# Block copies of turned squares on ScalarE instead of GpSimd, in a two-layer decoder trunk

## The chip, the cores and the metric

The kernel runs on one core of one Trainium2 chip. The metric is the device time of one execution in microseconds; the time before is the median of three runs, 2173.76 us (2171.62 to 2175.25).

## The reference

A decoder trunk of two layers on 256 tokens of width 2048, in fp32. Each layer is a token mixer and a gated feed-forward block with a short convolution:

```
h = h + gla_mixer(h, ...)                    # layer 0: gated linear attention, 4 heads
h = h + conv_ffn(h, ...)
k_blk, v_blk, k_mean = shared_kv(h, ...)     # layer 1: attention with 16 heads, causal, one block of 256
h = h + moba_mixer(h, ...)
h = h + conv_ffn(h, ...)

def conv_ffn(x, norm_w, w_up, conv_w, conv_b, w_down):
    h = rms_norm(x, norm_w) @ w_up           # (256, 2048) @ (2048, 11264)
    hp = pad(h, 2 rows in front)
    acc = conv_b
    for j in range(3): acc = acc + conv_w[j] * hp[:, j:j + S]
    a, u = split(acc, 2, axis=-1)
    return (silu(a) * u) @ w_down            # (256, 5632) @ (5632, 2048)
```

The convolution runs over tokens, and the products with the weights run over features.

## The kernel before

**Weights.** Every weight is streamed once from HBM, in chunks of 128 x 2048 fp32 (`wraw`, three buffers, loads on SyncE's queue, line L107). A chunk is two halves of 128 x 1024. For each half ScalarE makes a rounded high part (`whi`, L145), and VectorE subtracts it from the half to make the low part (`wlo`, L147). Both have four buffers. TensorE multiplies with the high part (L382), then with the low part (L385). One half is one step: `step` calls the jobs that are due, `WeightStream.prefetch` issues the parts some two halves ahead, and the products of the half follow.

**Groups.** `gemm_tok` makes a group of 512 output columns for both 128-token tiles, tokens on partitions, in eight steps of 12 matmuls. `ffn` has 22 groups in each layer (`up`); the gate of layer 0 has three such groups (`gate`), and each layer's output projection three (`out`).

**The turn.** What follows needs features on partitions and tokens along the free dimension. So after a group `turn_up` copies its two PSUM tiles to `up` on ScalarE (L761), VectorE transposes each in blocks of 32 x 32 (`uT`, L763), and `square` moves the blocks to their places: 16 copies, each from one 32-partition row of blocks to another, 32 x 256 elements (L395), on GpSimd. In [128, 2, 512] that is one copy for each pair of source quadrant m and target quadrant c. `squares` does the same for `gate` and `out` (L402). With three gate groups, six out groups and 44 up groups there are 53 x 16 = 848 copies.

**After the turn.** Eight and eleven steps later `conv` works on the two halves of the group: on ScalarE a scaled copy (`au`, L776), on VectorE two multiply-adds for each of two rows (L781, L783); one step on `gate` does the Silu on ScalarE (L789), the product on VectorE (L791), a rounded copy on ScalarE (`hid`, L423) and the subtraction on VectorE (L424). For some groups VectorE also makes sums of these (`comb`, L712 to L715), and GpSimd's queue stores them (`aside`, L735).

**Sums made ahead.** The down projection uses sums of weight blocks. `make_ahead` loads a chunk every nine steps (`ahead`, L333, SyncE's queue), VectorE makes four sums in it (L330, L331), and GpSimd's queue stores it (`tsum`, L340).

**What sets the order.** Each engine takes its instructions in order. A scheduler places them by priority from the program's order; `after_high()` and `after_low()` tell it to put an instruction behind the latest high or low part that was issued:

```
    def after_high():
        return tc.issue_after(ws.high.ins)
```

Waits between engines are by semaphores, in the order of each queue.

Of the kernel before, what the change touches and what calls it, by code (L numbers as in the profile page):

```python
# [159 lines left out]
def trunk(ctx: ExitStack, tc: tile.TileContext, xT, cst, msk, w1p, w2a, w_k, w_qa, w_v2, w_v, w_gt, w_g, w_got, w_go,  # L160
          w_up0, w_dn0, w_kk, w_kv, w_mq, w_mot, w_mo, w_up1, w_dn1, rel, onehot, out):
    nc = tc.nc
    V, A, T = nc.vector, nc.scalar, nc.tensor
# [181 lines left out]
    def after_high():  # L345
        return tc.issue_after(ws.high.ins)
# [43 lines left out]
    def square(y, x):  # L390

        for m in range(4):
            xs_ = x[32 * m:32 * m + 32].rearrange("a t (n c b) -> a n t c b", c=4, b=32)
            for c in range(4):
                nc.gpsimd.tensor_copy(y[32 * c:32 * c + 32, :, :, 32 * m:32 * m + 32], xs_[:, :, :, c])  # L395

    def squares(name, xs):

        x, y = slot([128, 2, 512], F32, name + "T"), slot([128, 4, S], F32, name)
        for t in range(2):  # L400
            with after_low():
                V.transpose(x[:, t], xs[t])  # L402
        square(y.rearrange("p n (t s) -> p n t s", t=2), x)
        return y
# [343 lines left out]
    def ffn(layer, nrm, then):  # L748
# [6 lines left out]
        def turn_up(g, ps):  # L755

            x = slot([128, 2, 512], F32, "uT")
            us = [temp("up", (128, 512)) for _ in range(2)]
            for t in range(2):
                with after_high():  # L760
                    A.activation(us[t], ps[:, t, :], AF.Copy, scale=nrm.col[:, t:t + 1])  # L761
                with after_low():
                    V.transpose(x[:, t], us[t])  # L763
            y = slot([128, 2, 2, S], F32, "up")
            square(y.rearrange("p j i (t s) -> p (j i) t s", t=2), x)
            for jj in range(2):
                after(UP_LAG[jj], lambda jj=jj: conv(g, jj, y[:, jj]))
# [505 lines left out]
```

## Time and profile before

| | |
|---|---|
| runs | 2171.62, 2173.76, 2175.25 us; median 2173.76 |
| profiled execution, first to last instruction (span) | 2171.2 us; no other time is given for it |
| TensorE (PE) busy | 2162.0 us, 9936 matmuls |
| VectorE (DVE) busy | 1839.8 us |
| ScalarE (ACT) busy | 1301.2 us |
| GpSimd (POOL) busy | 771.9 us |
| the 704 up copies on POOL (L395) | 521.2 us busy, mean 740 ns, 391 at the least and 1469 at the most |
| granted TensorE clock | 1.000 |

The span is what the timeline and the windows count from; the fastest run is 0.4 us above it. A busy share is a mean over the span: TensorE is near 100% in every slice of the page. A row of a group names line, engine, operation, written and read tiles and shapes, then busy time, mean duration, and the engine's idle time before it with what ended that.

### The profile page before, as it was taken

To read this page: it belongs to the slowest core of one execution; us is meant where nothing else is said; L and a number is where in the kernel's file an instruction comes from. 1 tells how busy PE (TensorE), PEld (TensorE's weight loads), DVE (VectorE), ACT (ScalarE), POOL (GpSimd) and SP (SyncE) were. 2 spreads that over 40 slices of the span, in tenths; PEclk is the share of its full clock that TensorE was granted. 3 is DMA by queue.
4 is the path that set the end of the run, shared out by engine and by line. 5 is a ranking of instruction groups with operands and counts; after the bars stand their busy time and mean duration, and the time that the engine had idled before them with its cause. 6 is when DMAs were issued, how large, how long until landed. Compare 5 with 4: busy or idle time off the path is not lost.

```text
span 2171.2 us, 28783 instructions
## 1 busy us (share of the span) xinstructions
PE 2162.0 (100%) x9936; PEld 1800.0 (83%) x9936; DVE 1839.8 (85%) x2525; ACT 1301.2 (60%) x1840; POOL 771.9 (36%) x1069
## 2 busy tenths in 40 slices
PE   9999999999999999999999999999999999999998
PEld 7888888888888888887888888888888888888887
DVE  6686788799999897978968787588999999979798
ACT  6655545556565655766756666455565656567575
POOL 0000347364656464300001343153555565552000
PEclk9999999999999999999999999999999999999999
DMA  7575577877778785887967788767788878759896
GB/s 287 210 291 210 217 280 284 325 265 283 275 284 309 275 311 192 328 329 260 367 246 291 276 300 292 254 253 286 279 308 284 305 279 296 290 191 352 323 359 248
DMA packets 113525, 612.99 MB, mean 282 GB/s; under 512 B 29361, under 2 KB 29889, under 8 KB 49634
## 3 DMA queue, kind: packets, MB, share of 16 engines
q1 hardware_dynamic: 94610, 523.75, 66.4%
q0 software_dynamic: 18048, 86.60, 10.5%
q8 instruction: 78, 1.28, 0.2%
q10 hardware_dynamic: 720, 0.79, 0.1%
q14 instruction: 69, 0.57, 0.1%
HBM read 535.31 MB, written 75.78 MB: 281 GB/s over the span
## 4 chain that ended last, share of the span: by engine, by line
PE 97%; DMA 1%; DVE 1%; issue 0%; ACT 0%; ACTq 0%; DVEq 0%
PE acc L382 46%; PE acc L385 23%; PE acc L844 13%; PE p L844 5%; PE acc L367 5%; PE acc L369 2%; DMA ahead<-tsum 1%; DMA wraw<-w_dn 1%; PE sT L594 0%; DVE wlo L147 0%; PE tr L1046 0%; PE s L1064 0%; DMA h<-xT 0%; ACT whi L145 0%; PE z L500 0%
## 5 line engine op out<-in xcount | busy, mean ns | idle before, releaser
L147 DVE TENSOR_TENSOR wlo<-wraw,whi 128x1024 fp32r<-128x1024 f32 (+1 forms) x788 | 959.8, 1226 | 251.7 <-ACT whi L145 202.7
L145 ACT CAST whi<-wraw 128x1024 fp32r<-128x1024 f32 (+1 forms) x788 | 795.5, 1016 | 608.7 <-PE acc L382 434.5
L382 PE MATMUL acc<-whi,xw 128*128 128x512 f32 x3520 | 873.0, 390 | 0.6 <-DVE xw L262 0.6
L382 PEld LDWEIGHTS acc<-whi,xw 128*128 128x128 f32 x3520 | 659.3, 188 | 138.0 <-issue 1.3
L395 POOL COPY up<-uT 32x256 f32<-32x256 f32 x704 | 521.2, 740 | 297.2 <-DVE uT L763 234.6
L385 PE MATMUL acc<-wlo,xw 128*128 128x512 f32 x1760 | 472.5, 389 | 0.0
L385 PEld LDWEIGHTS acc<-wlo,xw 128*128 128x128 f32 x1760 | 330.1, 188 | 68.6 <-DVE wlo L147 0.3
L340 POOL DMA_DIRECT2D tsum<-ahead x58 | 31.6, 545 | 453.0 <-DVE ahead L331 433.5
L844 PE MATMUL acc<-whi,hid 128*128 128x512 f32 x588 | 168.1, 390 | 1.7 <-ACT whi L145 1.7
L147 DVE TENSOR_TENSOR wlo<-ahead,whi 128x1024 fp32r<-128x1024 f32 x98 | 120.0, 1231 | 19.1 <-ACT whi L145 10.7
L844 PEld LDWEIGHTS acc<-whi,hid 128*128 128x128 f32 x588 | 109.8, 188 | 25.2 <-ACT whi L145 2.8
L382 PE MATMUL acc<-whi,xkv 128*128 128x512 f32 x512 | 129.9, 391 | 0.0
L145 ACT CAST whi<-ahead 128x1024 fp32r<-128x1024 f32 x98 | 101.5, 1052 | 42.1 <-PE p L844 16.6
L844 PE MATMUL p<-whi,hid 128*128 128x512 f32 x356 | 111.6, 389 | 0.0
L382 PEld LDWEIGHTS acc<-whi,xkv 128*128 128x128 f32 x512 | 95.1, 188 | 18.9
L844 PE MATMUL acc<-whi,comb 128*128 128x512 f32 x348 | 101.3, 390 | 0.5 <-ACT whi L145 0.5
L844 PE MATMUL acc<-wlo,hid 128*128 128x512 f32 x294 | 96.3, 390 | 0.0
L776 ACT ACTIVATE au<-up,cs 128x256 f32<-128x256 f32 x176 | 95.8, 593 | 0.0
L783 DVE SCALAR_TENSOR_TENSOR au<-up,cs,au 128x254 f32<-128x254 f32 x176 | 89.7, 540 | 0.0
L781 DVE SCALAR_TENSOR_TENSOR au<-up,cs,au 128x255 f32<-128x255 f32 x176 | 89.0, 542 | 0.2
L331 DVE TENSOR_TENSOR ahead<-ahead 128x512 f32<-128x512 f32 x116 | 87.0, 750 | 0.3
L330 DVE TENSOR_TENSOR ahead<-ahead 128x512 f32<-128x512 f32 x116 | 86.9, 750 | 0.3
(282 smaller groups left out, 2363.6 us busy)
## 6 DMA issues: line engine op xcount, KB each, us to landing
wraw<-w_up SPq DMA_DIRECT2D x176, 1024.0 KB, 5.5
ahead<-w_dn SPq DMA_DIRECT2D x58, 1024.0 KB, 8.8
tsum<-ahead POOLq DMA_DIRECT2D x58, 1024.0 KB, 8.3
ahead<-tsum SPq DMA_DIRECT2D x49, 1024.0 KB, 6.8
wraw<-w_dn SPq DMA_DIRECT2D x58, 768.0 KB, 6.2
wraw<-w_dn SPq DMA_DIRECT2D x30, 1024.0 KB, 6.3
wraw<-w_mq SPq DMA_DIRECT2D x16, 1024.0 KB, 5.0
wraw<-w_kk SPq DMA_DIRECT2D x16, 1024.0 KB, 5.3
```

Source lines behind the costliest of these rows:

```text
L145: self.high = nc.scalar.copy(hi[:, a:b], src[:, a:b])
L147: self.low = nc.vector.tensor_sub(lo[:, a:b], src[:, a:b], hi[:, a:b].bitcast(F32))
L330: jobs = [lambda: V.tensor_sub(b22, b22, b12), lambda: V.tensor_sub(b12, b12, b11), lambda: V.tensor_add(b11, b22, b11), lambda: V.tensor_ ...
L331: lambda: V.tensor_add(b11, b22, b11), lambda: V.tensor_sub(b21, b21, b11)]
L367: T.matmul(ps[:, b, :], two[i][0][:, c:c + 128], xs(kt), start=kt == 0, stop=False)
L382: T.matmul(ps[:, t, :], xs(kt)[:, x0 + 128 * t:x0 + 128 * t + 128], hi[:, c:c + 512], start=kt == 0 and x0 == 0, stop=False)
L385: T.matmul(ps[:, t, :], xs(kt)[:, 128 * t:128 * t + 128], lo[:, c:c + 512], start=False, stop=kt == KT - 1)
L395: nc.gpsimd.tensor_copy(y[32 * c:32 * c + 32, :, :, 32 * m:32 * m + 32], xs_[:, :, :, c])
L776: A.activation(au[:, i, :], t[:, i, :], AF.Identity, bias=col(cb + n), scale=col(cw + 2 * 2 * FT + n))
L781: V.scalar_tensor_tensor(au[:, i, 1:], t[:, i, :S - 1], col(cw + 2 * FT + n), au[:, i, 1:], op0=OP.mult, op1=OP.add)
L783: V.scalar_tensor_tensor(au[:, i, 2:], t[:, i, :S - 2], col(cw + n), au[:, i, 2:], op0=OP.mult, op1=OP.add)
L844: T.matmul(p[n], x[xi], w[wi][:, 512 * f:512 * f + 512], start=n not in begun, stop=left[n] == 0)
```

## The change

The 16 copies of `square` are issued to ScalarE, each behind the latest high part.

```diff
         for m in range(4):
             xs_ = x[32 * m:32 * m + 32].rearrange("a t (n c b) -> a n t c b", c=4, b=32)
             for c in range(4):
-                nc.gpsimd.tensor_copy(y[32 * c:32 * c + 32, :, :, 32 * m:32 * m + 32], xs_[:, :, :, c])
+                with after_high():
+                    A.copy(y[32 * c:32 * c + 32, :, :, 32 * m:32 * m + 32], xs_[:, :, :, c])
```

Every line behind it has a number one higher in the changed kernel (L395 is L396, L423 is L424, L776 is L777).

ScalarE's queue around the turn of the twentieth up group of layer 0; the `up` rows are the copies out of PSUM, `au` and `hid` belong to earlier groups. Before:

```order
L145 CAST whi<-wraw 128x1024
L761 ACTIVATE up<-acc,col_h 128x512 x2
L789 ACTIVATE au<-au 128x256
L145 CAST whi<-wraw 128x1024
L776 ACTIVATE au<-up,cs 128x256 x2
L423 CAST hid<-au 128x256
L145 CAST whi<-wraw 128x1024
L789 ACTIVATE au<-au 128x256
L145 CAST whi<-wraw 128x1024 x2
```

The same place in the changed kernel:

```order
L145 CAST whi<-wraw 128x1024
L762 ACTIVATE up<-acc,col_h 128x512 x2
L790 ACTIVATE au<-au 128x256
L145 CAST whi<-wraw 128x1024
L777 ACTIVATE au<-up,cs 128x256 x2
L396 COPY up<-uT 32x8x32 x16
L424 CAST hid<-au 128x256
L145 CAST whi<-wraw 128x1024
L790 ACTIVATE au<-au 128x256
L145 CAST whi<-wraw 128x1024 x2
```

The 16 copies stand in one piece between two casts; the `hid` cast and the next high part are behind them.

VectorE's queue at the same turn, from the low part ahead of the transposes. Before:

```order
L147 TENSOR_TENSOR wlo<-wraw,whi 128x1024
L763 STREAM_TRANSPOSE uT<-up 128x512 x2
L791 TENSOR_TENSOR au<-au 128x256
L147 TENSOR_TENSOR wlo<-wraw,whi 128x1024
L781 SCALAR_TENSOR_TENSOR au<-up,cs,au 128x255 x2
L424 TENSOR_TENSOR hid<-au,hid 128x256
L783 SCALAR_TENSOR_TENSOR au<-up,cs,au 128x254
L147 TENSOR_TENSOR wlo<-wraw,whi 128x1024
L783 SCALAR_TENSOR_TENSOR au<-up,cs,au 128x254
L147 TENSOR_TENSOR wlo<-wraw,whi 128x1024
```

The same place in the changed kernel:

```order
L147 TENSOR_TENSOR wlo<-wraw,whi 128x1024
L764 STREAM_TRANSPOSE uT<-up 128x512 x2
L792 TENSOR_TENSOR au<-au 128x256
L147 TENSOR_TENSOR wlo<-wraw,whi 128x1024
L782 SCALAR_TENSOR_TENSOR au<-up,cs,au 128x255 x2
L784 SCALAR_TENSOR_TENSOR au<-up,cs,au 128x254 x2
L425 TENSOR_TENSOR hid<-au,hid 128x256
L147 TENSOR_TENSOR wlo<-wraw,whi 128x1024
L792 TENSOR_TENSOR au<-au 128x256
L147 TENSOR_TENSOR wlo<-wraw,whi 128x1024 x2
L425 TENSOR_TENSOR hid<-au,hid 128x256
L147 TENSOR_TENSOR wlo<-wraw,whi 128x1024 x3
```

The first `hid` subtraction, which needs ScalarE's `hid` cast, has moved behind all four multiply-adds; the second low part after the transposes stands behind it.

## Prediction

> **What bounds the kernel now.** I read the page's busy times and chain first, then PE's list of waits.
>
> ```profile
> PE 2162.0 (100%) x9936; PEld 1800.0 (83%) x9936; DVE 1839.8 (85%) x2525; ACT 1301.2 (60%) x1840; POOL 771.9 (36%) x1069
> PE 97%; DMA 1%; DVE 1%; issue 0%; ACT 0%; ACTq 0%; DVEq 0%
> PE acc L844 <- ACT whi L145: 2.3, 4, 1.5
> PE junk L219 <- POOL idle L216: 1.3, 1, 1.3
> PE acc L385 <- DVE wlo L147: 0.7, 1, 0.7
> PE acc L382 <- DVE xw L262: 0.6, 1, 0.6
> PE acc L382 <- ACT whi L145: 0.3, 1, 0.3
> ```
>
> A row of waits gives us in total, times, and the longest. PE is busy 2162.0 of 2171.2 us and all its waits together are 5.2 us. No edit that leaves the products alone can win more than the 9.2 us in which PE is idle, and most of that is not behind these copies. The question is whether the moved work makes PE wait. 704 of the 848 copies belong to the 44 groups of the two up projections, so I read one group in the timeline, and the window 410 to 870, which holds 21.
>
> ```profile
> 410.00:870.00 460.00, 460.00 (x2031) 381.04 (x2030) 417.90 (x574) 276.03 (x394) 259.37 (x362) 1.00 0.75 275
> 627.01 1.04 ACT L145 CAST whi<-wraw 128x1024 fp32r<-128x1024 f32 x1
> 627.29 1.98 PE L382 MATMUL acc<-whi,xw 128*128 128x512 f32 x8
> 627.54 1.30 DVE L763 STREAM_TRANSPOSE uT<-up 128x512 f32<-128x512 f32 x2
> 628.97 12.73 POOL L395 COPY up<-uT 32x256 f32<-32x256 f32 x16 [7.43 <-DVE uT L763]
> 629.31 1.06 ACT L145 CAST whi<-wraw 128x1024 fp32r<-128x1024 f32 x1 [0.26 <-PE acc L382]
> 629.66 1.41 DVE L147 TENSOR_TENSOR wlo<-wraw,whi 128x1024 fp32r<-128x1024 f32 x1
> 630.01 1.98 PE L382 MATMUL acc<-whi,xw 128*128 128x512 f32 x8
> ```
>
> In the window row the columns after the length are PE, PEld, DVE, ACT, POOL: PE 460.00 of 460, DVE 417.90 (91%), ACT 276.03 (60%), POOL 259.37 (56%). PE's steps start 2.72 us apart (627.29, 630.01), so a group of eight is 21.76 us. The cast at 629.31 starts as PE ends the high products at 629.27: with four buffers it writes the high part for four steps on. ACT is thus as far ahead as the buffers let it, and it can be held for a while before PE notices.
>
> **Part 1: POOL loses the copies.** POOL's 12.73 us of each group go; nothing waits for POOL in PE's list, so this alone is worth nothing to PE. Its stores of `ahead` and `aside`, which stood behind copies, are issued sooner: nothing again, a buffer is free earlier. What it does change is DVE:
>
> ```profile
> L147 DVE TENSOR_TENSOR wlo<-wraw,whi 128x1024 fp32r<-128x1024 f32 x168 | 221.9, 1322 | 41.3 <-ACT whi L145 39.5 <-PE acc L385 1.3
> L330 DVE TENSOR_TENSOR ahead<-ahead 128x512 f32<-128x512 f32 x30 | 24.0, 800 | 0.1
> L331 DVE TENSOR_TENSOR ahead<-ahead 128x512 f32<-128x512 f32 x32 | 25.4, 794 | 0.1
> L714 DVE TENSOR_TENSOR comb<-au 128x128 f32<-128x128 f32 x9 | 4.3, 478 | 0.0
> L781 DVE SCALAR_TENSOR_TENSOR au<-up,cs,au x176: 467/480/648, 427.5 to 1969.9; 128x255 f32<-128x255 f32 x176
> 398.66 2.35 DVE L147 TENSOR_TENSOR wlo<-wraw,whi 128x1024 fp32r<-128x1024 f32 x2
> 601.88 0.68 DVE L330 TENSOR_TENSOR ahead<-ahead 128x512 f32<-128x512 f32 x1
> 607.02 0.38 DVE L791 TENSOR_TENSOR au<-au 128x256 f32<-128x256 f32 x1
> 642.89 0.41 DVE L424 TENSOR_TENSOR hid<-au,hid 128x256 fp32r<-128x256 f32 x1
> ```
>
> Beside a POOL copy a wlo takes 1.41 (629.66), away from one two take 2.35 together, 1.22 and then 1.13; an `ahead` sum takes 0.80 on average and 0.68 alone. So without POOL DVE gets shorter. An L781 takes 0.47 at the least and 0.65 at the most, a multiply (L791) alone 0.38, a hid subtraction 0.41. In a row I take 0.08 off each, as the two wlo show: a wlo 1.14, an `ahead` sum 0.60, an L781 or L783 0.40, the transposes (1.30 the pair) 1.26, a multiply 0.30, a hid subtraction 0.34. One group without `ahead` work is then 8 x 1.14 + 1.26 + 4 x 0.40 + 2 x 0.30 + 2 x 0.34 = 13.3 us; with 62/21 = 2.9 `ahead` sums (1.8) and the sums of `comb` (nine of L714, and of each of its like, in 21 groups: 0.6 on average), 15.7; waits are not in it. That is a relief of 2 to 3 us a group, and it pays for part of what follows.
>
> **Part 2: ACT gets 16 copies in one piece.** The nearest rows for one copy:
>
> ```profile
> L568 ACT COPY kie<-kie 128x256 f32<-128x256 f32 x4 | 1.6, 406 | 4.1 <-DVE kie L567 4.1
> L423 ACT CAST hid<-au 128x256 fp32r<-128x256 f32 x88 | 35.5, 403 | 71.7 <-DVE au L791 71.7
> L776 ACT ACTIVATE au<-up,cs 128x256 f32<-128x256 f32 x176 | 95.8, 593 | 0.0
> 624.88 1.09 ACT L776 ACTIVATE au<-up,cs 128x256 f32<-128x256 f32 x2
> 66.13 0.40 ACT L507 CAST zst<-zaug 17x256 fp32r<-17x256 f32 x1
> 66.55 0.41 ACT L508 CAST zst<-zaug 17x256 fp32r<-17x256 f32 x1
> ```
>
> 256 elements take 0.40, on 128 partitions or 17. Usually the next instruction overlaps by 0.1 (two L776 of 0.593 in 1.09), which would make the block 16 x 0.31 = 5.0 us. But L507 and L508, which wait for nothing between them, start 0.42 apart, more than the 0.40 of the first: L508 writes from partition 32, L507 from 0. Every one of the 16 copies writes at another block of 32 partitions than the one before. I take 16 x 0.43 = 6.9 us. Bounds: 5.0, and 8.0 if pieces of 32 elements cost 0.50. The Trainium skill, "VectorE: DVE Perf Modes", section "Two Vector instructions with no wait between them", says that a VectorE instruction whose output starts in another 32-partition quadrant is held until the earlier ones end; it says so of VectorE only, the L507 and L508 rows say it of ScalarE.
>
> ACT's total is no problem: 276.03/21 = 13.1 us a group, plus 6.9, is 20.0 of 21.76. What counts is what stands behind the block in ACT's queue: the cast that makes the next high part. Count from the end of a group's last step. The last cast ahead of the block is of the fifth part on; it may start when PE has done the next step's high products, at 2.0, takes 0.96, and two L776 take 1.0: the copies start at 4.0. They end at 10.9, the hid cast at 11.2, the next cast at 12.25. PE wants that part, the sixth, after five steps, at 13.6. The margin is 1.35 us, for a group that begins on time, so one block alone does not stop PE. Two loops decide whether groups begin on time.
>
> **Part 3: the loop through DVE.** When the transposes are done, DVE has on average some 3.5 us to do and then waits for the hid cast behind the block. The copies run 6.9, the hid cast 0.3, the next cast 1.05, and then DVE still has seven wlo (8.0), a multiply (0.3), a hid subtraction (0.3), four L781/L783 (1.6) and the transposes (1.3) before the next block may start: 8.25 + 11.5 = 19.8 us with no `ahead` work, 2.0 below 21.76. Four `ahead` sums (2.4) and the `aside` sums (1.3) make 23.5, 1.7 above. The average group is 19.8 + 1.9 = 21.7: the loop is full. What is over in one group is carried to the next; counted through the 44 groups in their order, group by group with these prices, it passes the margin in five groups by 0.01 to 0.7 us, together 1.4, and by 2.4 in the eleventh, where only a multiply and a `comb` sum stand between DVE's transposes and its wait. Together 4 us. Bounds: nothing at 0.31 a copy; at 0.50 every group is about 1.0 over, 44 us.
>
> **Part 4: the loop through the loads.** `wraw` has three buffers of two parts; one comes free when DVE has made its second wlo. The first wlo behind the block is such a one. The last row is for w_up.
>
> ```profile
> wraw<-w_up SPq DMA_DIRECT2D x176, 1024.0 KB, 5.5
> ahead<-w_dn SPq DMA_DIRECT2D x58, 1024.0 KB, 8.8
> SPq L107 <- DVE wlo L147: 1673.7, 386, 8.6
> DMA to landing us min/median/max: 4.7/5.5/11.4
> ```
>
> SP's queue waits for these wlo all the time (1673.7 us in all), so a later wlo is a later load. Loop: copies 6.9, hid cast 0.3, cast 1.05, wlo 1.14, load 5.5, cast 1.05, wlo 1.14, four L781/L783 1.6, wlo 1.14, transposes 1.3: 21.1 us, 0.6 below the group. A load beside an `ahead` load (8.8) makes 24.4, 2.7 over, of which the margin of 1.35 takes half. Of four loads in a group one is in the loop, and an `ahead` load falls in three groups of four: I take one group in five, 44 x 0.2 x 1.35 = 12 us. Bounds: nothing (every such load 4.7 to 5.5), and 44 us (every such load half-way between the two rows, 7.15, so that the loop is 22.75 and each group 1.0 over).
>
> **The nine other blocks** (gate and out) have the same 6.9 us in ACT, beside fewer ACT and DVE instructions; margins of 1.3 us or more by the same count. I cost them at nothing; if PE's steps there show waits, 9 x 1 us at most.
>
> **Sum.** 4 + 12 = 16 us on the profiled execution, whose span of 2171.2 stands beside the fastest of the three runs (2171.62; the median is 2.6 above the span). 2171.6 + 16 = 2188 us. 0.2%, some 4.3 us, is about what a measurement of this kernel tells from no change.
>
> **Rivals.** *Hidden* (no change): the copies overlap by 0.1 as L776 does, or loads land in 5.5. Block 5.0, DVE loop 19.8 on the average group, load loop 19.2; no term left, 2172 to 2178. For it: wherever ACT stays on the same partitions its rows overlap; against it L507 and L508, the only pair that moves. The Trainium skill's "ScalarE: Activation LUTs", section "What ACT_TABLE_LOAD costs", speaks for this rival: it lets back-to-back instructions overlap by about 93 ns. By that the block is about 5 us and the time that of before. *The loops are as tight as the page's busiest rows* (much slower): a copy over 32-element pieces costs more than kie's 64-element pieces, 0.5 in place of 0.43. Block 8.0, average loop 22.8, 1.0 over in every group: 44 us, 2216. It decides from about 0.44 on. For it: no row here has such pieces in and out. *Faster*: DVE, freed of POOL, keeps wlo ahead of PE at the ends of the up stages; that can return some of PE's 5.2 us of waits and no more: 2168 at best. Against it: the largest of these waits is for ACT's whi, not for DVE.
>
> **How the numbers follow.** A loss of 4 to 30 us, as summed: 0.45. Hidden: 0.32. Over 30 us: 0.18. Faster: 0.05. The likeliest case gives 2188 and by itself 2178 to 2204. Over all cases the range runs from 2172, which leaves out the faster case and some of the hidden one, to 2217, which takes in the costlier copy. Faster 0.05, within 0.2% 0.32, slower 0.63.
>
> **What would show it.** Right: 848 COPY on ACT with 0.41 us each and starts 0.43 apart; POOL's 704 up copies gone; the wlo mean of the up stage down from 1.32 to about 1.22; ACT busy near 1301 + 848 x 0.43 = 1660 us; PE's list of waits with 10 to 20 us more, for whi and wlo, in the up stages; the waits of casts for `wraw` up. Wrong: starts 0.31 apart, or PE's waits still near 5 us (hidden); PE waiting in every group by 1 us (much slower).

## The result, and the profile after

The changed kernel takes 2199.59 us (median, 2197.1 to 2201.83) against 2173.11 us for the kernel before in the same comparison: 1.0122 times as long, 95% interval 1.0108 to 1.0136. That is 26.5 us slower. The profiled execution took 2197.1 us, with a span of 2195.3 us against 2171.2: 24.1 us to be found.

Busy times, from the page of the changed kernel:

```profile
PE 2169.1 (99%) x9936; PEld 1801.9 (82%) x9936; DVE 1714.2 (78%) x2525; ACT 1616.5 (74%) x2688; POOL 139.1 (6%) x221
```

PE's list of waits (us, times, the longest):

```profile
PE acc L382 <- ACT whi L145: 11.4, 8, 3.6
PE acc L845 <- ACT whi L145: 8.0, 4, 3.2
PE junk L219 <- POOL idle L216: 1.3, 1, 1.3
PE acc L382 <- DVE xw L262: 1.2, 1, 1.2
PE acc L382 <- ACT go L424: 0.4, 1, 0.4
```

POOL lost 633 us, ACT gained 315 and DVE got 126 us shorter; none of the totals is a bound. PE still is, but where it waited 5.2 us it now waits 22.3, nearly all of it for `whi`, the high part that ACT casts. Those for `whi` are twelve in all: the loss is in a dozen places, and right behind them, and not in a slower pace of every group. The window that the prediction read, now:

```profile
410.00:870.00 460.00, 455.96 (x2008) 375.99 (x2007) 358.81 (x565) 394.75 (x724) 14.73 (x28) 1.00 0.74 274
```

Two groups of instructions, with the idle time before them and what ended it:

```profile
L396 ACT COPY up<-uT 32x256 f32<-32x256 f32 x704 | 284.0, 403 | 20.4 <-DVE uT L764 12.5
L425 DVE TENSOR_TENSOR hid<-au,hid 128x256 fp32r<-128x256 f32 x88 | 37.0, 420 | 123.4 <-ACT hid L424 123.4
```

And two kinds of loads, with the median time to landing:

```profile
wraw<-w_up SPq DMA_DIRECT2D x176, 1024.0 KB, 6.3
ahead<-w_dn SPq DMA_DIRECT2D x58, 1024.0 KB, 9.1
```

DVE is now busy 359 of 460 us in the window, but over the whole execution it sits idle for 123.4 us ahead of the hid subtraction (L425), until the hid cast that stands behind the copies is done. The w_up loads take 6.3 us where they took 5.5. Three places in the timeline make most of the loss. First, the eleventh up group of layer 0:

```profile
625.57 1.05 ACT L145 CAST whi<-wraw 128x1024 fp32r<-128x1024 f32 x1 [1.94 <-DMA wraw<-w_up]
626.65 1.23 DVE L147 TENSOR_TENSOR wlo<-wraw,whi 128x1024 fp32r<-128x1024 f32 x1 [0.68 <-ACT whi L145]
...
631.15 1.30 DVE L764 STREAM_TRANSPOSE uT<-up 128x512 f32<-128x512 f32 x2
632.37 0.38 DVE L792 TENSOR_TENSOR au<-au 128x256 f32<-128x256 f32 x1
632.48 6.62 ACT L396 COPY up<-uT 32x256 f32<-32x256 f32 x16 [2.47 <-DVE uT L764]
632.79 0.29 DVE L715 TENSOR_TENSOR comb<-au 128x128 f32<-128x128 f32 x1
639.44 1.04 ACT L145 CAST whi<-wraw 128x1024 fp32r<-128x1024 f32 x1
639.57 0.43 DVE L425 TENSOR_TENSOR hid<-au,hid 128x256 fp32r<-128x256 f32 x1 [6.49 <-ACT hid L424]
640.53 2.12 PE L382 MATMUL acc<-whi,xw 128*128 128x512 f32 x8 [2.47 <-ACT whi L145]
```

ACT stood idle 1.94 us for a load, the low part of it came late too, the transposes ended 2.47 us after ACT was free for the copies, and the next cast comes 2.47 us too late for PE. Second, the seam between the last up group and the down stage of layer 0; layer 1 has the same (a wait of 3.18 again):

```profile
872.93 0.71 DVE L764 STREAM_TRANSPOSE uT<-up 128x512 f32<-128x512 f32 x1
873.67 6.62 ACT L396 COPY up<-uT 32x256 f32<-32x256 f32 x16 [0.54 <-DVE uT L764]
880.32 1.04 ACT L145 CAST whi<-ahead 128x1024 fp32r<-128x1024 f32 x1
881.42 0.79 PE L845 MATMUL acc<-whi,comb 128*128 128x512 f32 x1 [3.18 <-ACT whi L145]
882.01 0.63 PE L845 MATMUL p<-whi,hid 128*128 128x512 f32 x1
882.44 0.63 PE L845 MATMUL acc<-whi,comb 128*128 128x512 f32 x1
```

The window behind that wait (the granted clock is the third number from the end):

```profile
881.42:884.83 3.41, 3.41 (x8) 2.73 (x9) 3.41 (x6) 3.41 (x6) 0.00 (x0) 0.51 0.61 161
```

The last block of the up stage runs when PE is already in the down stage, and the cast that PE wants next stands behind it. After the wait the products start 0.43 us apart (882.01, 882.44) in place of 0.23: the window gives a granted clock of 0.51 for 3.4 us, which costs another 1.7 us. Third, a group of layer 1, where ACT stood idle 3.46 us ahead of a cast, and the block came right behind this cast and the next one:

```profile
1573.04 1.05 ACT L145 CAST whi<-wraw 128x1024 fp32r<-128x1024 f32 x1 [3.46 <-PE acc L385]
1576.43 6.62 ACT L396 COPY up<-uT 32x256 f32<-32x256 f32 x16
1584.79 3.55 PE L382 MATMUL acc<-whi,xw 128*128 128x512 f32 x8 [3.65 <-ACT whi L145]
```

The profile puts the idle time at 1573.04 down to PE's low products, but SyncE's queue shows a load behind it:

```profile
1560.91 4.76 SPq L916 DMA_DIRECT2D hscr<-hT  x8
1565.77 0.40 SPq L107 DMA_DIRECT2D wraw<-w_up  x1
```

The chunk that the cast reads was asked for at 1565.77, behind eight stores of another tensor (`hscr`), and landed 7.17 us later, at 1572.94, 0.1 us ahead of the cast.

Each of PE's 9936 products can be set against the one of the same number in the kernel before. By that the up stages lose about 15.5 us (5.4 in layer 0, 10.1 in layer 1, of which 1.7 are half clock) and the two seams about 10 (twice 5.0, of which 1.7 each are half clock). The stages between and behind them win 1.5 back: 24.1 us together.

### The profile page after: what moved, and what is told of

The parts are those of the page before. It is cut to its first block, busy times and chain, and to the rows that moved or that the text cites. A ratio compares the mean times of both kernels' runs of the same rounds, so it can differ in the third digit from the quotient of the medians.

```text
span 2195.3 us, 28711 instructions
## 1 busy us (share of the span) xinstructions
PE 2169.1 (99%) x9936; PEld 1801.9 (82%) x9936; DVE 1714.2 (78%) x2525; ACT 1616.5 (74%) x2688; POOL 139.1 (6%) x221
## 4 chain that ended last, share of the span: by engine, by line
PE 64%; ACT 3%; DMA 2%; DVE 2%; issue 1%; SPq 0%; DVEq 0%; ACTq 0%
PE acc L382 29%; PE acc L385 14%; PE acc L845 13%; PE p L845 5%; ACT up L396 2%; DMA wraw<-w_up 1%; PE acc L367 1%; DVE wlo L147 1%; ACT whi L145 1%; DMA wraw<-w_dn 1%; DMA sums<-tsum 0%; SPq L916 0%; PE acc L369 0%; PE tr L1047 0%; PE s L1065 0%
## 5 line engine op out<-in xcount | busy, mean ns | idle before, releaser
L147 DVE TENSOR_TENSOR wlo<-wraw,whi 128x1024 fp32r<-128x1024 f32 (+1 forms) x788 | 914.3, 1174 | 241.2 <-ACT whi L145 198.8
L145 ACT CAST whi<-wraw 128x1024 fp32r<-128x1024 f32 (+1 forms) x788 | 784.3, 1013 | 374.0 <-PE acc L382 207.1
L382 PE MATMUL acc<-whi,xw 128*128 128x512 f32 x3520 | 875.8, 390 | 11.8 <-ACT whi L145 10.6
L382 PEld LDWEIGHTS acc<-whi,xw 128*128 128x128 f32 x3520 | 659.3, 188 | 153.6 <-ACT whi L145 16.3
L396 ACT COPY up<-uT 32x256 f32<-32x256 f32 x704 | 284.0, 403 | 20.4 <-DVE uT L764 12.5
L425 DVE TENSOR_TENSOR hid<-au,hid 128x256 fp32r<-128x256 f32 x88 | 37.0, 420 | 123.4 <-ACT hid L424 123.4
L382 PE MATMUL acc<-whi,xkv 128*128 128x512 f32 x512 | 129.9, 391 | 0.0
L382 PEld LDWEIGHTS acc<-whi,xkv 128*128 128x128 f32 x512 | 95.1, 188 | 18.9
L777 ACT ACTIVATE au<-up,cs 128x256 f32<-128x256 f32 x176 | 96.0, 593 | 0.0
L845 PEld LDWEIGHTS acc<-whi,comb 128*128 128x128 f32 x348 | 65.5, 189 | 21.3 <-ACT whi L145 7.8
L330 DVE TENSOR_TENSOR ahead<-ahead 128x512 f32<-128x512 f32 x116 | 79.4, 684 | 3.5 <-DMA ahead<-w_dn 3.3
L845 PEld LDWEIGHTS p<-whi,hid 128*128 128x128 f32 x356 | 67.7, 190 | 14.2
```

The source lines that it names most:

```text
L145: self.high = nc.scalar.copy(hi[:, a:b], src[:, a:b])
L147: self.low = nc.vector.tensor_sub(lo[:, a:b], src[:, a:b], hi[:, a:b].bitcast(F32))
L330: jobs = [lambda: V.tensor_sub(b22, b22, b12), lambda: V.tensor_sub(b12, b12, b11), lambda: V.tensor_add(b11, b22, b11), lambda: V.tensor_ ...
L382: T.matmul(ps[:, t, :], xs(kt)[:, x0 + 128 * t:x0 + 128 * t + 128], hi[:, c:c + 512], start=kt == 0 and x0 == 0, stop=False)
L396: A.copy(y[32 * c:32 * c + 32, :, :, 32 * m:32 * m + 32], xs_[:, :, :, c])
L425: V.tensor_sub(dst_lo, src, dst_hi.bitcast(F32))
```

## The experiments

### Only the last block of each layer back on GpSimd

```diff
-    def square(y, x):
+    def square(y, x, pool=False):
...
+                if pool:
+                    nc.gpsimd.tensor_copy(y[32 * c:32 * c + 32, :, :, 32 * m:32 * m + 32], xs_[:, :, :, c])
+                    continue
...
-            square(y.rearrange("p j i (t s) -> p (j i) t s", t=2), x)
+            square(y.rearrange("p j i (t s) -> p (j i) t s", t=2), x, g == FT // 2 - 1)
```

> The copies of the last up group of each layer go back to GpSimd, the other 51 blocks stay on ScalarE. Seam theory (16 copies in one piece hold the casts that the faster down steps need at once; the two waits of 3.3 us and the half clock of 3.4 us behind each cost 10 us of the 26): 2189 us, and no TensorE wait at the two seams. Full-loop theory (the loss is spread over the groups as the two loops are full): 2199 us, since two groups of 44 carry a twentieth of it.

Measured 2189.22 us (2188.01 to 2190.37), 1.0079 times the kernel before (1.0064 to 1.0094). PE's waits:

```profile
PE acc L382 <- ACT whi L145: 9.8, 8, 4.1
PE acc L848 <- ACT whi L145: 1.7, 2, 1.1
```

That is 17.2 us over the kernel before, 9.3 less than the changed kernel: two blocks of 44 made more than a third of the loss, near the 10 us read from the two seams. The down stage's waits fall from 8.0 to 1.7 us, the up stages' stay (9.8 against 11.4).

### The blocks in four pieces, two steps apart

```diff
-        for m in range(4):
+        for m in rows:
...
-            square(y.rearrange("p j i (t s) -> p (j i) t s", t=2), x)
+            y4 = y.rearrange("p j i (t s) -> p (j i) t s", t=2)
+            square(y4, x, (0,))
+            for m in (1, 2, 3):
+                after(2 * m, lambda m=m: square(y4, x, (m,)))
```

> The 16 copies of an up group stay on ScalarE but are issued in four pieces of four, two steps apart, each behind a later high part. Work on every engine is as in the changed kernel. Head-of-line theory (what costs is the piece of 6.6 us in front of the next cast): 2173 to 2178 us, TensorE's waits back to some 5 us. Full-loop theory (ScalarE's and VectorE's work and mutual waits add up to a group's time): 2195 to 2203 us, as the work is the same. Late-load theory (a wraw load that lands late, whatever the copies do): about 2190 us.

Measured 2176.61 us (2174.78 to 2178.89), 1.0022 times (1.0012 to 1.0031). Busy times:

```profile
PE 2164.3 (100%) x9936; PEld 1798.8 (83%) x9936; DVE 1726.7 (79%) x2525; ACT 1628.3 (75%) x2688; POOL 140.3 (6%) x221
```

PE's waits:

```profile
PE acc L848 <- ACT whi L145: 2.4, 4, 1.2
PE acc L382 <- ACT whi L145: 0.5, 1, 0.5
```

Part of one group's copies in the timeline:

```profile
500.62 0.82 ACT L396 COPY up<-uT 32x256 f32<-32x256 f32 x2
501.46 1.05 ACT L145 CAST whi<-wraw 128x1024 fp32r<-128x1024 f32 x1
502.54 1.65 ACT L396 COPY up<-uT 32x256 f32<-32x256 f32 x4
504.21 0.42 ACT L793 ACTIVATE au<-au 128x256 f32<-128x256 f32 x1
```

ACT and DVE do as much as in the changed kernel (1628.3 against 1616.5, and 1726.7 against 1714.2), and 22 of the 26.5 us are gone: a cast, `501.46`, now stands between two pieces. The work on ACT costs next to nothing; that casts stand behind 6.6 us of it in one piece costs the time.

### The two loops of a block exchanged

```diff
-            xs_ = x[32 * m:32 * m + 32].rearrange("a t (n c b) -> a n t c b", c=4, b=32)
-            for c in range(4):
+            for n in range(4):
+                c = m
+                xs_ = x[32 * n:32 * n + 32].rearrange("a t (n c b) -> a n t c b", c=4, b=32)
...
-                    A.copy(y[32 * c:32 * c + 32, :, :, 32 * m:32 * m + 32], xs_[:, :, :, c])
+                    A.copy(y[32 * c:32 * c + 32, :, :, 32 * n:32 * n + 32], xs_[:, :, :, c])
```

> The same 16 copies with the loops exchanged: four in a row write the same 32 partitions and read from four different ones. If only a change of the output's partitions takes the overlap away, 12 of 16 starts are 0.31 apart, a block is 5.4 us in place of 6.6, and by the head-of-line theory each of some dozen TensorE waits is 1.2 us shorter: 2184 to 2189 us. If a change of the input's partitions takes it away as well, starts stay 0.41 apart and the time stays 2197 to 2202 us.

Four copies in a row now write the same partitions and read four different ones. Measured 2201.31 us (2199.03 to 2202.16), 1.0134 times (1.0117 to 1.0151). A block:

```profile
435.48 6.62 ACT L397 COPY up<-uT 32x256 f32<-32x256 f32 x16
```

6.62 us as before the exchange, so 0.41 from start to start: reading elsewhere takes the overlap away as writing elsewhere does.

### The nine blocks of gate and out alone on ScalarE

With the first experiment's `square`:

```diff
-            square(y.rearrange("p j i (t s) -> p (j i) t s", t=2), x)
+            square(y.rearrange("p j i (t s) -> p (j i) t s", t=2), x, True)
```

> Only the nine blocks of gate and out are on ScalarE; the 704 up copies are back on GpSimd. The trace of the changed kernel shows 1.7 us of new TensorE waits there, so 2175 us by it. The prediction costed these at nothing: 2173 us. Over 2178 us would be neither.

Measured 2172.27 us (2171.74 to 2173.88), 1.0001 times (0.9992 to 1.0011): no difference. PE's waits add up to 5.0 us, as before the change.

### Half the bytes in the loads ahead

The `ahead` parts of the down projection are loaded during the up stages; here half of each is.

```diff
-                nc.sync.dma_start(t, ws.rows(w, at[0], 2048 * at[1]))
+                nc.sync.dma_start(t[:, :1024], ws.rows(w, at[0], 2048 * at[1])[:, :1024])
```

> The changed kernel, whose loads of the down projection's parts beside the up stages bring half the bytes (512 KB less every nine steps; DVE makes as many sums, on the half that was loaded, and the same bytes are stored; the down projection's sums are then not the reference's). Late loads set the waits at 442, 1533, 1581 and 1649 us (the load loop of the prediction): these 1.7 + 1.0 + 3.8 and 1.7 of half clock + 1.6 = about 10 us go, the casts' waits for wraw fall from 26.2 to under 12 us; the seams (10 us) and the eleventh group (2.6) stay: 2187 to 2191 us. Rival, the loads are late beside the waits and not behind them (DVE and the block alone set them): 2197 to 2200, with PE's waits for whi near those of the changed kernel (19 us).

Measured 2199.25 us (2197.42 to 2201.55), 1.0120 times (1.0103 to 1.0136): no gain. The waits of PE in the up stages (a line number there is four higher), the casts' waits for w_up, and the loads:

```profile
PE acc L386 <- ACT whi L145: 9.9, 11, 1.8
```

```profile
ACT whi L145 <- DMA wraw<-w_up: 32.2, 18, 3.0
```

```profile
wraw<-w_up SPq DMA_DIRECT2D x176, 1024.0 KB, 5.8
ahead<-w_dn SPq DMA_DIRECT2D x58, 512.0 KB, 7.5
```

The loads land sooner (w_up 5.8 in place of 6.3), but the casts wait longer for them (32.2 in place of 26.2), and PE's up waits fall only from 11.4 to 9.9. Of the waits of 1.56, 2.47 and 3.65 us that began at 442, 638 and 1581 us in the changed kernel the first is gone and the others are smaller (1.05 and 1.72), but others of 1 to 2 us stand at other groups. Part of what they saved was lost elsewhere (2.0 us more of waits in the attention stage, and 1 us more of half clock at the first seam), so a small gain isn't excluded; the 10 us expected are.

### One VectorE sum of four on each part loaded ahead

```diff
-            for i, job in enumerate(jobs):
+            for i, job in enumerate(jobs[:1]):
```

> The changed kernel with one of the four VectorE sums of each loaded down-projection part, and all loads and stores (three quarters of the sums are left out, so the down projection isn't the reference's). DVE has 3 x 0.68 = 2.0 us less to do in three groups of four. DVE theory for the eleventh group alone: its wait at 637 us (2.6) goes, the others stay: 2195 to 2198 us. Rival, the loop through DVE is full in every group and is behind all waits of the up stages: 15 us go, 2183 to 2187. Second rival, the eleventh group too is set by a load: 2198 to 2201.

Measured 2191.53 us (2189.65 to 2194.98), 1.0089 times (1.0074 to 1.0104). PE's waits, and the casts' for w_up:

```profile
PE acc L845 <- ACT whi L145: 9.5, 5, 3.2
PE acc L382 <- ACT whi L145: 2.6, 4, 0.9
```

```profile
ACT whi L145 <- DMA wraw<-w_up: 26.0, 20, 2.6
```

The casts wait for loads as long as before (26.0), and yet PE's waits in the up stages fall from 11.4 to 2.6 us, in layer 0 to nothing. Product against product, the up stages lose 4.0 us in place of 15.5. The whole loss fell by 7 us only, because waits in the attention and down stages grew (one of 2.1 us at 2129 is new, with half clock behind it) and the half clock at the first seam lasted 6.8 us in place of 3.4. The time is between the ranges of the theories; the waits of the up stages are those of the rival, a loop through DVE that is full everywhere. At the third place of above the cast stood idle 2.64 us for a load here as well, and yet PE lost 1.1 us there in place of 5.4. Without these sums some other ACT and DVE instructions change places too, so the next but one experiment, which keeps the order, counts for more.

### The eleventh block on GpSimd as well

With the first experiment's `square`:

```diff
-            square(y.rearrange("p j i (t s) -> p (j i) t s", t=2), x)
+            square(y.rearrange("p j i (t s) -> p (j i) t s", t=2), x, g in (10, FT // 2 - 1))
```

> The changed kernel with the last block of each layer and the eleventh back on GpSimd. Against the kernel with the last block alone there (2189.2 us) the wait at 637 us and the half clock after it go: 2.2 + 1.7 = 4 us, so 2184 to 2187 us. Rival, what the eleventh group lacks is carried on and comes out in the next group: 2188 to 2191.

Measured 2185.94 us (2185.56 to 2187.46), 1.0062 times (1.0047 to 1.0077): 13.7 us over the kernel before, 3.5 less than with the last blocks alone. The eleventh block of both layers has moved. The wait at 638 us is gone, and with it the half clock behind it (3.9 us together in the kernel with the last blocks alone); waits of 0.5 and 0.5 us came up in later groups of layer 0, and half of the 3.9 us was lost again there. Layer 0's up stage loses 4.9 us in place of 6.2, and the rest of the gain is in layer 1 (8.1 in place of 9.8): the time is that of the theory, but the rival is right in part.

### The same copies, with partitions that stay

```diff
-                    A.copy(y[32 * c:32 * c + 32, :, :, 32 * m:32 * m + 32], xs_[:, :, :, c])
+                    A.copy(y[32 * m:32 * m + 32, :, :, 32 * c:32 * c + 32], xs_[:, :, :, c])
```

> The changed kernel with each block's copies written to the partitions that they read (32m to 32m + 31 in place of 32c to 32c + 31), so that four in a row stay on the same partitions both ways; order, counts and sizes are the same, only the squares stay unturned, so the output isn't the reference's. Theory of the tight loop: starts inside a run of four fall to 0.31, a block to 16 x 0.31 + 3 x 0.1 = 5.3 us, 1.3 less on ACT and in the loop through DVE; the up stages' 15 us of waits fall to 3 or less, each seam's wait from 3.18 to 1.9: 2178 to 2185 us. Rival, the hidden case as the prediction priced it (a block of 5 us costs nothing): 2172 to 2177. Second rival, any two 32-partition copies fail to overlap, whichever partitions they use: starts 0.41 as before, 2197 to 2201.

Measured 2180.01 us (2178.91 to 2181.1), 1.0035 times (1.0021 to 1.0048). A block, and PE's waits:

```profile
497.00 5.31 ACT L396 COPY up<-uT 32x256 f32<-32x256 f32 x16
```

```profile
PE acc L845 <- ACT whi L145: 5.5, 5, 1.9
PE acc L382 <- ACT whi L145: 1.3, 3, 0.8
```

With every instruction of PE, ACT, DVE and POOL in its place in the order and 1.3 us less in each block, 18.6 of the 26.5 us are gone (7.9 are left): the up stages' waits fall from 11.4 to 1.3, each seam's from 3.18 to 1.87. Product against product, the up stages lose 1.0 us in place of 15.5, and each seam 4.4 in place of 5.0. This is the run that settles it: with a block of 5.3 us the loops of the up stages have room, at 6.6 they don't.

### Reading and writing at different, constant partitions

```diff
-                    A.copy(y[32 * c:32 * c + 32, :, :, 32 * m:32 * m + 32], xs_[:, :, :, c])
+                    A.copy(y[32 * (3 - m):32 * (4 - m), :, :, 32 * c:32 * c + 32], xs_[:, :, :, c])
```

> As the kernel that writes each block's copies where they read, but written to the opposite 32 partitions (read 32m, write 32(3 - m)): four copies in a row read the same partitions and write the same, other ones. The order is that of the changed kernel; the squares stay unturned, so the output isn't the reference's. Theory: what takes the overlap away is that a copy changes its partitions against the one before: starts 0.31 inside a run of four, block 5.3 us, 2178 to 2185 us, as with read and written partitions equal (2180.0). Rival: a copy that writes at other partitions than it reads can't overlap: starts 0.41, block 6.6, 2197 to 2201.

Measured 2180.86 us (2180.16 to 2181.84), 1.0043 times (1.0026 to 1.0060). A block, and the group of all up copies:

```profile
496.59 5.32 ACT L396 COPY up<-uT 32x256 f32<-32x256 f32 x16
```

```profile
L396 ACT COPY up<-uT 32x256 f32<-32x256 f32 x704 | 232.9, 400 | 10.7 <-DVE uT L764 8.3
```

A copy that writes elsewhere than it reads overlaps as well: 5.32 = 12 x 0.307 + 3 x 0.41 + 0.40. What takes the overlap away is the change against the copy before.

### Both terms taken out: last blocks on GpSimd, one sum of four

With the first experiment's `square`, called as there:

```diff
-            for i, job in enumerate(jobs):
+            for i, job in enumerate(jobs[:1]):
...
-            square(y.rearrange("p j i (t s) -> p (j i) t s", t=2), x)
+            square(y.rearrange("p j i (t s) -> p (j i) t s", t=2), x, g == FT // 2 - 1)
```

> The changed kernel with the last block of each layer back on GpSimd, and one of the four VectorE sums of each loaded down-projection part (three quarters of these sums are left out, so the down projection isn't the reference's). If the two seams and the loop through DVE are all of the loss: up stages 3 us or less of waits, no wait at the seams, a few us in the down stages as with the one sum alone: 2176 to 2181 us. Rival, the seam's wait turns up again at the next high part, or the late loads (casts' waits for wraw still near 26 us) cost by themselves: 2184 to 2190.

Measured 2180.56 us, with a wide spread (2175.23 to 2184.32), 1.0034 times (1.0020 to 1.0047). The profile shows no wait at the seams, 4.0 us at L382, and a wait of 3.0 us in the attention stage that the changed kernel hasn't; it was taken of the longest execution. The median is in the theory's range, the spread reaches into the rival's.

## Why the prediction was right or wrong

**Direction and kind: right.** Slower, in the likeliest case (a loss of 4 to 30 us); the time was 11.6 us above the number given and inside the range.

**Part 1, POOL's relief: right.** A wlo by itself takes 1.22 us and POOL is down to 139 us. In the window PE was busy for all of the 460 us before, so nothing of that could win it time there. DVE's relief is 2.8 us a group (417.9 to 358.8 us in 21 groups), within the 2 to 3 that the prediction gives. Its sum for an average group, 15.7 us, doesn't fit that, though: 17.1 were measured, and from the 19.9 of before 15.7 would be a relief of 4.2.

**Part 2, the block: right.** 6.62 us measured, 6.9 predicted, since the copies do not overlap. The rule cited from the Trainium skill ("VectorE: DVE Perf Modes", section "Two Vector instructions with no wait between them") has a VectorE instruction held for where its input starts, too, and not only for its output; the exchanged loops and the two kernels with constant partitions show ScalarE to behave by both. The rival *Hidden*, which rested on an overlap of 0.1, was wrong on that, and not quite right on the price either: with most of the overlap given back (a block of 5.3 us, where the rival has 5.0) there is still 8 us of loss, 0.35%: two seams of 4.4 us each with their half clock.

**The margin of 1.35 us: right for the up stages, not looked at elsewhere.** PE waits for a high part in 7 of the 42 other up groups, so one block alone doesn't stop it there. The margin was counted with PE's pace of the up stage. The step that failed is the one that priced "44 groups" by one pace: the last block of each layer runs beside the down stage, whose products use up the high parts faster (in the kernel before ACT makes 77 in the 130 us from 870 on, one in 1.7 us, and one in 2.7 us from 410 to 860), and there one block alone stops PE. Two blocks made some 10 us, for which the sum had no term.

**Part 3, the loop through DVE: right in kind and at the eleventh group (2.4 predicted, 2.5 of waiting measured), too small as a term.** It gave 4 us; with 1.3 us less in the loop the up stages' waits are gone, so nearly all of the 15.5 us depends on this loop and the margin behind the block, both of which that shortens or widens; 2.0 us less on DVE alone took 8.8 of the 11.4 us of waits. **Part 4, the loads: too large as a term by the one run that bears on it.** It gave 12 us to `ahead` loads beside w_up loads; half their bytes took away 1.5 us of PE's waits in the up stages. The casts waited longer for loads in that run, though, so what punctual loads are worth was not measured. At the costliest group (5.4 us at 1585) the late load stood behind `hscr` stores on SyncE's queue, which the prediction didn't count. The two loops were priced apart and added, though they are one: the rows of the eleventh group show a late load, then a late low part, late transposes and a late block. That a load's delay costs only where DVE has no slack to take it up is the reading that fits: less work on DVE removed the waits with the loads as late as ever. It was not shown by a run with the loads alone made punctual. That the two terms came to 16 us and the up stages to 15.5 is two errors that cancel.

**The nine blocks at nothing: right,** by a kernel with them alone. **The half clock** after PE's waits, 5 us in all, was not in the prediction.

## What to carry to other kernels

Before giving an engine more work, look at what stands behind it in its queue, and for how long in one piece: the same copies cost 26.5 us with up blocks of 6.6 us and 4.5 us with the up blocks in four pieces of 1.7. Count the margin anew at the seams between stages, where the consumer's pace changes, and do not price loops apart that share a buffer. A run of ScalarE instructions on parts of the partitions is shorter if neighbours keep their 32-partition blocks.

## What the runs showed of the hardware

- ScalarE instructions overlap by 0.09 us (starts 0.307 apart, 0.400 long) as long as each reads and writes in the same 32-partition blocks as the one before; a change of either makes the starts 0.41 apart.
- PE's granted clock fell to half for 3.4 us after waits of 3.18, 3.65 and 3.18 us, but not after the 2.47 us that ended at 641 us (the first two windows below, of the changed kernel); in the kernel with one sum of four it fell after one of 2.09 us, too (the third). The first seam has a wait of 1.87 us both in the kernel with partitions that stay (the fourth window: 0.50) and in the one that reads and writes at different ones (the fifth: 1.00), and only the former has half clock behind it. So the length of the wait alone doesn't decide it. The Trainium skill, "TensorE: Matmul & The Clock Gate", section "What's actually happening", puts the half clock behind an idle window of about 3.4 us that runs free; the length of 3.4 us agrees, the waits that it came behind here are partly shorter.

```profile
1584.80:1588.20 3.40, 3.40 (x9) 2.68 (x10) 3.40 (x5) 3.08 (x4) 0.00 (x0) 0.54 0.00 0
640.50:644.00 3.50, 3.47 (x15) 2.89 (x16) 3.49 (x5) 3.50 (x5) 0.00 (x0) 1.00 0.00 0
```

```profile
2128.50:2132.90 4.40, 4.02 (x12) 3.10 (x13) 3.98 (x7) 4.40 (x8) 0.00 (x0) 0.69 1.01 414
```

```profile
875.67:879.08 3.41, 3.17 (x8) 2.44 (x8) 3.41 (x6) 3.08 (x5) 0.48 (x1) 0.50 0.89 297
```

```profile
873.30:880.00 6.70, 6.39 (x26) 4.66 (x27) 6.70 (x10) 6.70 (x11) 0.53 (x1) 1.00 0.75 222
```
